# Handing out 32 DRAM-to-DRAM weight sums one at a time behind split weight operands

## The chip, the cores and the metric

The kernel runs on one core of one Trainium2 chip. The metric is the device time of one execution in microseconds (us); the figure quoted is the median of several executions.

## The reference, cut to what matters

The reference is one decoder layer with float32 weights: a normalised input projection (`w_in`), a causal 31-tap depthwise convolution with layer norm beside a multi-head latent attention of 8 heads, a gated merge and an output projection, a cross-attention on 256 memory tokens, and a squared-ReLU MLP, followed by a final RMS norm. The part that the change concerns is the second MLP product:

```python
u = rms_norm(h, norm_mlp_g[l])
h = h + jnp.square(jax.nn.relu(u @ w_mlp1[l])) @ w_mlp2[l]
```

`w_mlp2` has 4096 rows and 1024 columns. The kernel cuts it into four blocks B11, B12, B21, B22 (2048 rows by 512 columns each) and forms the product with seven block products instead of eight (a Strassen-Winograd scheme). For that it needs four sums of weight blocks, which it makes at run time.

## The kernel before, in words

**Matmuls.** Every float32 operand is split into a high and a low float32r part by `split` (lines 225 to 227): ScalarE (ACT) casts the high part, `wh`, and a second engine subtracts to get the low part, `wl`. `mm3` (lines 261 to 263) then issues three matmuls for each tile: high by high, high by low, low by high. A weight chunk is loaded by SP into one of two `raw` buffers (`raw`, line 362; usually 1 MB), and `prep` splits it piece by piece into one of three `wh`/`wl` pairs. The second engine of a weight split is `w_eng[0]`: VectorE (DVE) for chunk 1, GpSimd (POOL) from the second projection chunk to the cross-attention, and DVE again from the cross-attention's output projection on. `Pipe.unit` prepares the next unit's operand before it emits the matmuls of the unit before.

**Stages.** In the profiled execution TensorE (PE) works through: the start, in which `x` and the first weight chunk arrive (0 to 26 us); the projections `ag`, `cq`, `ckv` and 16 gate units, with the convolution's taps on DVE beside them (to 223); the attention (to 330); the merge's output projection, 8 units (to 375); the memory cross-attention (to 470); the first MLP product, 32 units (`m1`, to 650); and the seven block products (`m2`, to 825).

**The sums.** `b_sums_gen` (lines 322 to 342) makes the four sums X, V, Y, Z in DRAM, each in four pieces of 1 MB. For a piece c there are four copies from DRAM to DRAM and four DMAs with an accumulate: X = B12 + B11, V = B12 + B22, then Y = B11 + V and Z = B21 + Y. These are 32 DMAs of 1 MB on the queue of POOL, since POOL issues them. The `m2` stage reads X first, at 670.9 us.

**Order.** Only PE's order is that of the program text. The instructions of the other engines are ordered by a scheduler, which may take an instruction earlier than the text has it when nothing that it needs holds it back. The text asks for one sum DMA after each of the 8 units of the output projection and for two after each pass of the `m1` loop (`b_sums`, called at lines 1075 and 1266). The copies depend on no computed data and the accumulating DMAs only on earlier sum DMAs, and the scheduler has put all 32 among POOL's first instructions: the first two are issued at 1.4 and 2.1 us and the last at 172.5 us.

Of the kernel before, what the change touches and what calls it, by code (L numbers as in the profile page):

```python
# [14 lines left out]
F32 = mybir.dt.float32  # L15
# [4 lines left out]
ALU = mybir.AluOpType  # L20
# [3 lines left out]
P = 128  # L24
# [168 lines left out]
def _body(tc, a):  # L193
# [5 lines left out]
    gps = nc.gpsimd  # L199

    def pool(name, bufs=1, side=None, space=None):
        kw = dict(name=name, bufs=bufs, reuse_waits="tile")
        if side:
            kw["side"] = side
        if space:
            kw["space"] = space
        cm = tc.tile_pool(**kw)
        return cm, cm.__enter__()
# [5 lines left out]
    cst_cm, cst = pool("cst")  # L214
# [5 lines left out]
    def bank(tag="mm"):  # L220
        nonlocal ps
        return ps.tile([P, S], F32, tag=tag, name=tag, bufs=PB[tag])


    def split(hi, lo, src, eng=None):
        act.copy(hi, src)  # L226
        (eng or dve).tensor_tensor(lo, src, hi.bitcast(F32), op=ALU.subtract)  # L227
# [27 lines left out]
    def mm3(out, pairs, first=True, last=True, again=False):  # L255

        n = len(pairs)
        cols = out.shape[-1] / S
        for i, ((wh, wl), (ah, al)) in enumerate(pairs):
            kw = dict(skip_group_check=True) if again else {}  # L260
            pe.matmul(out, wh, ah, start=first and i == 0, stop=False, **kw)  # L261
            pe.matmul(out, wh, al, start=False, stop=False, **kw)  # L262
            pe.matmul(out, wl, ah, start=False, stop=last and i == n - 1, **kw)  # L263
            tick(cols)
# [48 lines left out]
    sums = {(n, c): spp.tile([P, 2048], F32, name="%s_%d" % (n, c)) for n in SUMS for c in range(4)}  # L313
# [4 lines left out]
    def chunk_hbm(i):  # L318
        n = stream[i][3] * len(stream[i][4])
        return a["weights"][offs[i]:offs[i] + P * n].rearrange("(p n) -> p n", p=P)  # L320

    def b_sums_gen():

        src = lambda *key: chunk_hbm(ch[key])
        b11, b22, b21 = ((lambda c, n=n: src("m2", n, c)) for n in (0, 3, 5))
        b12 = lambda c: src("b12", c)
        start = lambda c: [(("x", c), b12(c)), (("v", c), b12(c)), (("y", c), b11(c)), (("z", c), b21(c))]
        adds = lambda c: [(("x", c), b11(c)), (("v", c), b22(c)), (("y", c), sums["v", c]),
                          (("z", c), sums["y", c])]
        steps = [(start(c), False) for c in range(4)]  # L330
        for c in range(4):
            for d, s_ in start(c):
                gps.dma_start(out=sums[d], in_=s_)
                yield
            if c > 0:
                for d, s_ in adds(c - 1):
                    gps.dma_start(out=sums[d], in_=s_, accum_op=ALU.add, max_dma_last_dim=8192)
                    yield
        for d, s_ in adds(3):
            gps.dma_start(out=sums[d], in_=s_, accum_op=ALU.add, max_dma_last_dim=8192)  # L340
            yield

    b_gen = b_sums_gen()

    def b_sums(n):
        for _ in range(n):
            next(b_gen, None)

    def raw(*key):
        ci = ch[key]  # L350
        while issued[0] < len(stream) and issued[0] < ci + RAW_BUFS:
            i = issued[0]
            _, _, _, kt, cols = stream[i]
            n = kt * len(cols)
            t = wp.tile([P, 2048], F32, tag="raw", name="raw", bufs=RAW_BUFS)
            src = sums[stream[i][1], stream[i][2]] if stream[i][1] in SUMS else chunk_hbm(i)
            raws[i] = t[:, :n].rearrange("p (k m) -> p k m", k=kt)
            if i == 1:
                for sl in (slice(0, 128), slice(128, 256)):
                    dma(out=raws[i][:, :, sl], in_=src.rearrange("p (k m) -> p k m", k=kt)[:, :, sl])  # L360
            else:
                dma(out=t[:, :n], in_=src)
            issued[0] += 1
        return raws[ci]

    def whl(kt, cols):
        hi = wp.tile([P, 1024], F32R, tag="wh", name="wh", bufs=3)
        lo = wp.tile([P, 1024], F32R, tag="wl", name="wl", bufs=3)
        return tuple(t[:, :kt * cols].rearrange("p (k m) -> p k m", k=kt) for t in (hi, lo))

    def prep(key, k0=0, kt=None, c0=0, cols=128):

        r = raw(*key)
        kt = r.shape[1] if kt is None else kt
        hi, lo = whl(kt, cols)
        split(hi, lo, r[:, k0:k0 + kt, c0:c0 + cols], w_eng[0])
        return hi, lo

    w_eng = [dve]
# [100 lines left out]
    n = NT * 16  # L480
# [176 lines left out]
    for k in range(KD):  # L657
# [9 lines left out]
        for i, j in ((0, 0), (1, 0), (0, 1)):  # L667
            for b, c0 in ((fa, 0), (fg, 128)):
                pe.matmul(b, hl[i][:, k % 4, c0:c0 + 128], (uh, ul)[j][:, k, :],
                          start=k == 0 and i == j == 0, stop=k == KD - 1 and j == 1)  # L670
        tick(2.0)
    pipe.ahead(lambda: prep(("ag", 1), c0=0))
    x_stats()

# [121 lines left out]
    def qkt(tag):  # L796
        return at.tile([P, 2, S], F32R, tag=tag, name=tag, bufs=QB)
# [17 lines left out]
    def k_pair(p):  # L815
        b = bank()
        c = slice(128 * p, 128 * p + 128)
        mm3(b, [((wkk[:, 0, k, c], wkk[:, 1, k, c]), (ckh[:, k, :], ckl[:, k, :])) for k in range(2)])
        for e in range(2):
            n = slice(64 * e, 64 * e + 64)  # L820
            rr = slice(64 - 64 * e, 128 - 64 * e)
            kt_ = qkt("k")
            split(kt_[n, 0, :], kt_[n, 1, :], b[n, :])
            act.copy(kt_[rr, 0, :], krh[rr, :].bitcast(F32))
            act.copy(kt_[rr, 1, :], krl[rr, :].bitcast(F32))
            ks[2 * p + e] = kt_
# [51 lines left out]
        return prep(("co", p // 2), c0=256 * (p % 2), cols=256)  # L878

    hq = None  # L880
    k_pair(0)
    for t in range(NT):
        b = bank()
# [182 lines left out]
    def out_unit(m):  # L1066
        def main(hl):
            b = bank()
            mm3(b, [(lhs(hl, k), (mgh[:, k, :], mgl[:, k, :])) for k in range(KD)])
            n1.add(m, b)  # L1070
        pipe.unit(lambda: prep(("wo", m // 2), c0=128 * (m % 2)), main)

    for m in range(KD):
        out_unit(m)
        b_sums(1)
        if m == 2:
            mem_norm()
    for m in range(XH):
# [174 lines left out]
    def spill(m):  # L1253
        b = bank("at")
        for t in range(NT):
            pe.transpose(b[:, t * P:(t + 1) * P], ht[:, m, t * P:(t + 1) * P], ident)
        t_ = hop.tile([P, NT, P], F32, tag="spill", name="spill", bufs=2)
        act.copy(t_.rearrange("p t c -> p (t c)"), b)
        act.dma_start(out=hsp[:, m * P:(m + 1) * P].rearrange("(t p) c -> p t c", p=P), in_=t_)

    for p in range(16):
        for j in range(2):
            m1_unit(p, j)
        if 1 <= p <= KD:
            spill(p - 1)
        b_sums(2)


    m2w = {}
# [215 lines left out]
```

## Time and profile before

| | |
|---|---|
| Median of 3 executions | 829.14 us (828.45 to 829.21) |
| The profiled execution, its own time | 826.94 us |
| Its span (first to last instruction) | 825.0 us |
| PE busy | 769.2 us (93%) |
| DVE busy | 537.8 us (65%) |
| ACT busy | 400.4 us (49%) |
| POOL busy | 175.1 us (21%) |
| Moved by DMA | 129.58 MB, 33.56 MB of it on POOL's queue |

PE is busy for 93% of the span, so what can be won lies in the 56 us in which it is not, and in stretches in which it works at its lower clock. The page's second part shows the span in 40 equal slices of 20.6 us each: one line per engine, the clock granted to PE, the load of the 16 DMA engines and what they moved. A release (`<-`) behind an idle time names the work that ended it.

### The profile page before, as it was taken

The numbers are of one execution on the slowest core, as the hardware profiler recorded it, in microseconds if no ns is written. First come the engines' busy times: TensorE is split into PE (matmuls) and PEld (weight loads), VectorE is DVE, ScalarE is ACT, GpSimd is POOL, SyncE is SP. The second block draws the span as 40 slices with busy tenths as digits, with TensorE's granted clock in tenths as the row PEclk, the third lists the DMA queues.
The fourth block names the chain that finished last, engine by engine and source line by source line (L and its number), as shares of the span: only waits on it lengthen the run. The fifth ranks groups of instructions, "written<-read, shape, count | busy, mean of one in ns | idle before, by whom it ended". The sixth has DMA issues, their size and how long they took to land.

```text
span 825.0 us, 9536 instructions
## 1 busy us (share of the span) xinstructions
PE 769.2 (93%) x3594; PEld 632.5 (77%) x3594; DVE 537.8 (65%) x808; ACT 400.4 (49%) x681; POOL 175.1 (21%) x120
## 2 busy tenths in 40 slices
PE   5889974889999999899899999999999999999995
PEld 3679764777878888688887888888888878888884
DVE  3988977583378885976778663333333376677785
ACT  4432231236876653633446554444344455555563
POOL 3646271643322221434632000000000000000000
PEclk7999998899999999999999999999999999999999
DMA  8899999971220214421422123322322355555564
GB/s 296 334 257 325 307 294 220 253 210 52 90 89 1 103 52 147 160 91 66 150 103 102 51 103 128 122 87 110 115 103 102 121 186 203 177 210 200 187 220 154
DMA packets 27645, 129.58 MB, mean 157 GB/s; under 512 B 2640, under 2 KB 10192, under 8 KB 16208
## 3 DMA queue, kind: packets, MB, share of 16 engines
q1 hardware_dynamic: 16048, 85.37, 28.9%
q0 software_dynamic: 2816, 33.56, 15.3%
q10 hardware_dynamic: 8736, 10.06, 3.8%
q8 instruction: 28, 0.46, 0.2%
q14 instruction: 17, 0.14, 0.1%
HBM read 124.78 MB, written 37.75 MB: 197 GB/s over the span
## 4 chain that ended last, share of the span: by engine, by line
PE 66%; DVE 12%; issue 8%; DMA 7%; ACT 4%; POOL 3%; SPq 0%; POOLq 0%; DVEq 0%; ACTq 0%
PE mm L263 18%; PE mm L262 18%; PE mm L261 18%; DMA v<-weights 3%; PE at L262 2%; PE at L263 2%; PE at L261 2%; POOL wl L227 2%; DMA raw<-weights 2%; DMA xr<-xT 1%; DVE q L227 1%; DVE mt L964 1%; ACT wh L226 1%; PE at L857 1%; DVE wl L227 1%
## 5 line engine op out<-in xcount | busy, mean ns | idle before, releaser
L226 ACT CAST wh<-raw 128x1024 fp32r<-128x1024 f32 (+4 forms) x146 | 147.5, 1013 | 278.8 <-PE mm L262 148.8
L227 POOL TENSOR_TENSOR wl<-raw,wh 128x1024 fp32r<-128x1024 f32 (+4 forms) x65 | 148.5, 2300 | 211.6 <-ACT wh L226 208.4
L227 DVE TENSOR_TENSOR wl<-raw,wh 128x1024 fp32r<-128x1024 f32 x81 | 98.9, 1223 | 132.0 <-ACT wh L226 132.0
L261 PE MATMUL mm<-hgh,wh 128*128 128x512 f32 x288 | 113.2, 393 | 0.0
L262 PE MATMUL mm<-hgl,wh 128*128 128x512 f32 x288 | 112.2, 389 | 0.0
L263 PE MATMUL mm<-hgh,wl 128*128 128x512 f32 x288 | 112.2, 389 | 0.0
L263 PE MATMUL mm<-uh,wl 128*128 128x512 f32 x176 | 72.0, 409 | 12.6 <-POOL wl L227 9.8
L541 DVE SCALAR_TENSOR_TENSOR cv<-zpad,vec,cv 128x512 f32<-128x512 f32 x116 | 80.0, 746 | 0.1
L261 PE MATMUL mm<-uh,wh 128*128 128x512 f32 x176 | 72.4, 411 | 0.0
L262 PE MATMUL mm<-ul,wh 128*128 128x512 f32 x176 | 70.7, 402 | 0.0
L263 PEld LDWEIGHTS mm<-hgh,wl 128*128 128x128 f32 x288 | 54.1, 188 | 11.5
L262 PEld LDWEIGHTS mm<-hgl,wh 128*128 128x128 f32 x288 | 54.1, 188 | 10.9
L261 PEld LDWEIGHTS mm<-hgh,wh 128*128 128x128 f32 x288 | 54.1, 188 | 10.9
L263 PEld LDWEIGHTS mm<-uh,wl 128*128 128x128 f32 x176 | 34.5, 196 | 22.6 <-POOL wl L227 11.5
L1280 POOL MEMSET eps<- 128x1 f32 x1 | 0.1, 99 | 215.7 <-PE mm L263 215.7
L263 PE MATMUL mm<-wh,hB 128*128 128x512 f32 x100 | 39.6, 396 | 1.1 <-DVE hB L227 1.1
L261 PEld LDWEIGHTS mm<-uh,wh 128*128 128x128 f32 x176 | 34.6, 197 | 7.6 <-issue 1.0
L261 PE MATMUL mm<-wh,hA 128*128 128x512 f32 x100 | 39.6, 396 | 0.9 <-ACT hA L226 0.9
L262 PEld LDWEIGHTS mm<-ul,wh 128*128 128x128 f32 x176 | 34.7, 197 | 7.1
L262 PE MATMUL mm<-wl,hA 128*128 128x512 f32 x100 | 39.5, 395 | 0.0
L262 PE MATMUL at<-wl,hA 128*128 128x512 f32 x72 | 28.6, 397 | 0.3 <-DVE wl L227 0.3
L261 PE MATMUL mm<-mgh,wh 128*128 128x512 f32 x64 | 26.0, 406 | 3.1 <-ACT mgh L226 3.1
(384 smaller groups left out, 1696.1 us busy)
## 6 DMA issues: line engine op xcount, KB each, us to landing
raw<-weights SPq DMA_DIRECT2D x55, 1024.0 KB, 4.9
x<-weights POOLq DMA_DIRECT2D x4, 1024.0 KB, 18.7
v<-weights POOLq DMA_DIRECT2D x4, 1024.0 KB, 18.6
y<-v POOLq DMA_DIRECT2D x4, 1024.0 KB, 9.2
z<-y POOLq DMA_DIRECT2D x4, 1024.0 KB, 9.7
raw<-x SPq DMA_DIRECT2D x4, 1024.0 KB, 4.8
raw<-y SPq DMA_DIRECT2D x4, 1024.0 KB, 4.9
raw<-v SPq DMA_DIRECT2D x4, 1024.0 KB, 4.8
```

Source lines behind the costliest of these rows:

```text
L226: act.copy(hi, src)
L227: (eng or dve).tensor_tensor(lo, src, hi.bitcast(F32), op=ALU.subtract)
L261: pe.matmul(out, wh, ah, start=first and i == 0, stop=False, **kw)
L262: pe.matmul(out, wh, al, start=False, stop=False, **kw)
L263: pe.matmul(out, wl, ah, start=False, stop=last and i == n - 1, **kw)
L541: dve.scalar_tensor_tensor(run if w < CW - 1 else acc[:, c, :], zs, wcol, run, op0=ALU.mult, op1=ALU.add)
L857: pe.transpose(b[:, (t - k) * P:(t - k + 1) * P], ptok[h, t][:, k * P:(k + 1) * P], ident)
L964: dve.tensor_tensor(t, t, gates[:, m, :], op=ALU.add)
L1280: gps.memset(eps, EPS)
```

## The change

A one-element copy on POOL, `pace`, now stands ahead of every sum DMA. It reads an element of the `wl` that was just split, so it cannot run before that split, and `issue_after` puts the DMA behind the copy in POOL's order. `b_sums` is now called by `prep` after each split and counts up by `b_rate`: nothing before the attention, one DMA for every two splits from the attention on, and one for every split in `m1` but the first, whose operand is prepared ahead of the loop. Copies and accumulating DMAs are interleaved one by one, each accumulation a round later than the copy that it adds to, and V is added ahead of X.

```diff
-        adds = lambda c: [(("x", c), b11(c)), (("v", c), b22(c)), (("y", c), sums["v", c]),
+        adds = lambda c: [(("v", c), b22(c)), (("x", c), b11(c)), (("y", c), sums["v", c]),
                           (("z", c), sums["y", c])]
-        steps = [(start(c), False) for c in range(4)]
-        for c in range(4):
-            for d, s_ in start(c):
-                gps.dma_start(out=sums[d], in_=s_)
-                yield
-            if c > 0:
-                for d, s_ in adds(c - 1):
+        for c in range(5):
+            for n in range(4):
+                if c < 4:
+                    d, s_ = start(c)[n]
+                    gps.dma_start(out=sums[d], in_=s_)
+                    yield
+                if c > 0:
+                    d, s_ = adds(c - 1)[n]
                     gps.dma_start(out=sums[d], in_=s_, accum_op=ALU.add, max_dma_last_dim=8192)
                     yield
-        for d, s_ in adds(3):
-            gps.dma_start(out=sums[d], in_=s_, accum_op=ALU.add, max_dma_last_dim=8192)
-            yield
...
-    def b_sums(n):
-        for _ in range(n):
-            next(b_gen, None)
+    pace = cst.tile([P, 1], F32, name="pace")
+    b_rate, b_due = [0.0], [0.0]
+
+    def b_sums(lo):
+
+        b_due[0] += b_rate[0]
+        while b_due[0] >= 1.0:
+            b_due[0] -= 1.0
+            ins = gps.tensor_copy(pace, lo[:, 0, 0:1].bitcast(F32))
+            with tc.issue_after(ins.ins):
+                next(b_gen, None)
...
         split(hi, lo, r[:, k0:k0 + kt, c0:c0 + cols], w_eng[0])
+        b_sums(lo)
         return hi, lo
...
     hq = None
+    b_rate[0] = 0.5
     k_pair(0)
...
         out_unit(m)
-        b_sums(1)
...
+    b_rate[0] = 1.0
     for p in range(16):
...
-        b_sums(2)
```

Three places show what moves. The first is POOL's order in the projections, where `wl` of 128x768 belongs to `cq` and `wl` of 128x1024 to the gates. Before:

```order
L227 TENSOR_TENSOR wl<-raw,wh 128x1024 [waits PE_49,Activation_49]
L333 DMA x_82<-weights 16x16384 [waits DMASW2_49]
L227 TENSOR_TENSOR wl<-raw,wh 128x768 [waits DMAHW4_49,PE_49,Activation_49]
L337 DMA y_88<-v_84 128x2048 [waits DMASW3_49,DMASW1_49]
L333 DMA v_86<-weights 16x16384 [waits DMASW4_49]
L227 TENSOR_TENSOR wl<-raw,wh 128x768 [waits PE_49,Activation_49]
L337 DMA z_92<-y_88 128x2048 [waits DMASW5_49,DMASW3_49]
L227 TENSOR_TENSOR wl<-raw,wh 128x768 [waits DMAHW5_49,PE_49,Activation_49]
```

The same place after the change:

```order
L227 TENSOR_TENSOR wl<-raw,wh 128x1024 [waits PE_49,Activation_49]
L227 TENSOR_TENSOR wl<-raw,wh 128x768 [waits DMAHW4_49,PE_49,Activation_49]
L227 TENSOR_TENSOR wl<-raw,wh 128x768 [waits PE_49,Activation_49]
L227 TENSOR_TENSOR wl<-raw,wh 128x768 [waits DMAHW5_49,PE_49,Activation_49]
L227 TENSOR_TENSOR wl<-raw,wh 128x768 [waits Activation_49]
```

All sum DMAs are gone from here, and with them the waits on other sum DMAs (`DMASW`) that stood between two weight splits. The second place is POOL's order at the end of the output projection and in the memory keys (`xk`), after the change; before, only the `wl` rows stood there:

```order
L351 COPY pace<-wl 128x1 [waits Pool_49]
L338 DMA y_88<-v_84 128x2048 [waits DMASW5_49,DMASW2_49]
L227 TENSOR_TENSOR wl<-raw,wh 128x1024 [waits DMAHW7_49,PE_49,Activation_49]
L227 TENSOR_TENSOR wl<-raw,wh 128x1024 [waits PE_49,Activation_49]
L351 COPY pace<-wl 128x1 [waits Pool_49]
L334 DMA z_93<-weights 16x16384
L227 TENSOR_TENSOR wl<-raw,wh 128x1024 [waits DMAHW0_49,PE_49,Activation_49]
L227 TENSOR_TENSOR wl<-raw,wh 128x1024 [waits PE_49,Activation_49]
L351 COPY pace<-wl 128x1 [waits Pool_49]
L338 DMA z_92<-y_88 128x2048 [waits DMASW3_49,DMASW1_49]
L227 TENSOR_TENSOR wl<-raw,wh 128x1024 [waits DMAHW1_49,PE_49,Activation_49]
```

Between two sum DMAs there are two weight splits, and a sum that needs another one (`z_92` needs `y_88`) stands two DMAs behind it. In all, 16 sum DMAs now stand among POOL's weight splits and 16 behind splits that DVE makes. The third place is SP's order at the start. Before:

```order
L360 DMA raw<-weights 128x8x128 [waits DMAHW7_49]
L470 DMA kon<-konst 128x576 [waits DMAHW0_49]
L471 DMA posi<-positions 128x4 [waits DMAHW1_49]
L362 DMA raw<-weights 128x2048 [waits DMAHW2_49,DMAHW3_49,DVE_49,Pool_49]
L362 DMA raw<-weights 128x2048 [waits DMAHW7_49,DMAHW6_49,DVE_49]
```

After the change:

```order
L366 DMA raw<-weights 128x8x128 [waits DMAHW7_49]
L368 DMA raw<-weights 128x2048 [waits DMAHW0_49,DMAHW3_49,DVE_49,Pool_49]
L477 DMA kon<-konst 128x576 [waits DMAHW1_49]
L478 DMA posi<-positions 128x4 [waits DMAHW2_49]
L368 DMA raw<-weights 128x2048 [waits DMAHW7_49,DMAHW6_49,DVE_49]
```

The constants (`kon`) and the positions, from which DVE computes the rotary tables, now stand behind a weight load that waits until the first `raw` buffer is free.

## Rows read from the trace of the kernel before

**Rows 1.** The page's second part: tenths in 40 slices of 20.6 us
```profile
PE   5889974889999999899899999999999999999995
...
PEclk7999998899999999999999999999999999999999
DMA  8899999971220214421422123322322355555564
GB/s 296 334 257 325 307 294 220 253 210 52 90 89 1 103 52 147 160 91 66 150 103 102 51 103 128 122 87 110 115 103 102 121 186 203 177 210 200 187 220 154
```

**Rows 2.** The page's DMA queues (packets, MB, engine share) and issues (KB, median landing)
```profile
q1 hardware_dynamic: 16048, 85.37, 28.9%
q0 software_dynamic: 2816, 33.56, 15.3%
...
raw<-weights SPq DMA_DIRECT2D x55, 1024.0 KB, 4.9
x<-weights POOLq DMA_DIRECT2D x4, 1024.0 KB, 18.7
...
z<-y POOLq DMA_DIRECT2D x4, 1024.0 KB, 9.7
```

**Rows 3.** Timeline of POOL: start us, duration us, instruction, idle before it and releaser
```profile
1.44 0.67 POOL L333 DMA_DIRECT2D x<-weights  x1
...
22.99 0.52 POOL L333 DMA_DIRECT2D y<-weights  x1
...
81.20 1.34 POOL L337 DMA_DIRECT2D v<-weights  x1
...
141.76 0.81 POOL L337 DMA_DIRECT2D y<-v  x1 [19.00 <-DMA v<-weights]
```

**Rows 4.** Timeline of PE at the same place: start us, duration us, instruction
```profile
144.04 0.61 PE L262 MATMUL at<-wl,uh 128*128 128x288 f32 x1 [11.00 <-POOL wl L227]
```

**Rows 5.** The chain of waits, in order of time: start us, duration us, what
```profile
78.04 15.33 DMA raw<-weights
...
107.89 0.43 PE mm L261
...
111.46 0.23 PE mm L261
```

**Rows 6.** Three stretches of 10 us: stretch, length, busy us and instructions, PEclk, DMA, GB/s
```profile
100.00:110.00 10.00, 5.51 (x20) 3.99 (x19) 10.00 (x18) 5.03 (x8) 5.95 (x4) 0.88 0.92 233
140.00:150.00 10.00, 5.96 (x30) 5.96 (x30) 0.00 (x0) 0.54 (x1) 4.43 (x4) 0.57 1.02 213
180.00:190.00 10.00, 10.00 (x49) 8.25 (x48) 3.01 (x5) 3.66 (x5) 3.70 (x3) 1.00 0.47 182
```

**Rows 7.** Whole stages, same columns (PE, PEld, DVE, ACT, POOL busy)
```profile
44.00:223.00 179.00, 158.18 (x750) 133.50 (x749) 128.77 (x205) 68.70 (x117) 77.14 (x59) 0.94 0.81 226
330.00:375.00 45.00, 40.92 (x170) 32.32 (x169) 38.50 (x53) 22.91 (x36) 19.86 (x8) 0.96 0.33 120
375.00:440.00 65.00, 62.21 (x354) 53.88 (x353) 47.99 (x67) 30.31 (x58) 29.72 (x13) 1.00 0.28 98
470.00:650.00 180.00, 180.00 (x814) 149.02 (x813) 70.97 (x89) 81.30 (x143) 0.00 (x0) 1.00 0.30 106
```

**Rows 8.** Timelines of ACT, PE and DVE in the first 44 us
```profile
13.62 0.72 ACT L230 ACTIVATE uh<-xr,vec 128x512 fp32r<-128x512 f32 x1 [1.31 <-DMA xr<-xT]
14.39 1.22 PE L669 MATMUL mm<-uh,wh 128*128 128x512 f32 x2 [7.26 <-ACT uh L230]
...
39.07 3.11 DVE L273 TENSOR_TENSOR rs_t<-rs_t,rv 128x4 f32<-128x4 f32 x1
...
43.66 0.62 PE L295 MATMUL at<-kon,rx 128*128 128x128 f32 x4 [2.75 <-issue]
```

**Rows 9.** Timeline of DVE in the first MLP product: two weight splits in a row
```profile
502.84 1.22 DVE L227 TENSOR_TENSOR wl<-raw,wh 128x1024 fp32r<-128x1024 f32 x1 [4.72 <-ACT wh L226]
...
508.27 1.23 DVE L227 TENSOR_TENSOR wl<-raw,wh 128x1024 fp32r<-128x1024 f32 x1 [1.43 <-ACT wh L226]
```

## Prediction, made before the changed kernel ran

> **What bounds the kernel now.** I began with the page's slices. PE is the engine to watch, and it is full nearly everywhere except in the first nine slices, up to about 185 us [rows 1]. Exactly there the 16 DMA engines are full and move 210 to 334 GB/s; afterwards their load falls to a fifth or so. The queue table says what fills them: POOL's queue carries 33.56 MB, a quarter of all bytes, and all of it early [rows 2]. A 1 MB accumulation into X or V takes 18.7 us to land in this crowd, while the median weight load of 1 MB, taken over the whole kernel, needs 4.9 us.
>
> Next come the waits between engines, in two shapes. In the first, a weight load itself is late: one that the chain follows takes 15.33 us, from 78.04 on [rows 5]. In the second, POOL stands in its own queue: at 141.76 it issues Y = B11 + V after 19.00 us of waiting for V [rows 3], the split behind it in order is late, and PE resumes at 144.04 after 11.00 us without work [rows 4]. Whoever asks who is waiting for the sums themselves finds nobody: they are read only after 670 us.
>
> Last the price. From 44 to 223 us PE is busy for 158.18 of 179.00 us and its mean granted clock is 0.94 [rows 7]; from 180 to 190 us, with the sums over, it has no gap and runs at 1.00 [rows 6]. After a gap of some microseconds the granted clock is at the lower of its two levels, 1.2 instead of 2.4 GHz: from 107.89 matmuls of 512 columns step at 0.43 us, from 111.46 at 0.23 [rows 5].
>
> **The change, part by part.**
>
> *From 44 to 223 us.* All sum DMAs leave this stretch. The gaps are 179.00 - 158.18 = 20.8 us [rows 7]. To this come the recoveries at the lower clock: one lasts about 3.6 us (107.9 to 111.5), in which steps of 0.43 in place of 0.23 lose nearly half, 1.7 us [rows 5]. Between 90 and 180 us I count four such recoveries (two of them in the first two stretches of rows 6, with mean clocks of 0.88 and 0.57), so 4 x 1.7 = 6.8 us. The most that this stretch can give is 27.6 us. Is another engine next? DVE is busy for 128.8 us [rows 7], part of it held up by POOL, and PE would need 179.0 - 27.6 = 151 us, so DVE fits, if less loosely than it looks, as its work comes in bursts. POOL's 77.1 us shrink by some 28 DMA issues. I keep 3.6 us as left-over waits and take **24 us**. Ends: 14 (half stays, since DVE's bursts then end last) and 27.6.
>
> *The start.* Two sums are issued from 1.44 us on [rows 3], ahead of most of x. The second slice of x lets ACT start at 13.62 and PE at 14.39, after 7.26 us without work [rows 8]. Without those two megabytes x comes earlier. Against it stands SP's new order: the constants now wait behind a weight load that needs the first buffer free, and the rotary tables, the row statistics and the broadcast at 43.66 hang on them in DVE's order. That broadcast already cost PE 2.75 us, and one DVE step ahead of it took 3.11 us [rows 8] while POOL ran a split. The gain is between 0 (the constants take it all) and 7.26 + 2.75 = 10.0; I take the middle, **5 us**.
>
> *The 16 sums among POOL's weight splits (attention to cross-attention).* Each costs POOL an issue of 0.52 us for a copy or 0.81 us for an accumulation, plus the small `pace` copy, which no row shows; I put it at 0.15. That is 16 x (0.67 + 0.15) = 13 us of POOL time. POOL is busy for 19.9 of 45 us and 29.7 of 65 us in the two stages that hold most of them [rows 7], and the operand ring lets it work ahead, so most is hidden. If the cover were gone, all 13 would show. On the channel, a sum fills all 16 engines for 0.153 x 825 / 32 = 3.9 us and a weight load of 1 MB for 0.289 x 825 / 85.4 = 2.8 us [rows 2]. The output projection takes one of each for two units of 5.4 us, 6.7 of 10.8 us: loose. In the memory keys a unit has half the columns, so two loads and two sums, 13.4 us, meet some 11 us: loads can slip there by 2 to 3 us, in one or two places. What POOL waits for now is a sum two DMAs back, four splits earlier; behind it queue the splits of `xq`. I take 2 us for POOL and 2 us for the loads, **4 us lost**, between 0 and 21 (13 + 8).
>
> *The 16 sums behind DVE's splits (mostly `m1`).* Two splits there are 508.27 - 502.84 = 5.4 us apart [rows 9], and one sum follows each. In 10.9 us the channel gets one load and two sums, 2.8 + 7.8 = 10.6 us: as good as full, up from 0.30 [rows 7], for about 14 units. Then it empties again, near 550 us, and X is not read before 670. I cost this at nothing. The cover is that a weight load is asked for about two units before its split, against 4.9 us to landing [rows 2], and that PE has no gap there now [rows 7]. POOL does nothing else in this stage. If a `pace` copy is late, it holds one of the three `wl` buffers, and DVE's split three units on waits for it. The `pace` copies that run on after the last sum queue behind nothing.
>
> *The sum.* 24 + 5 - 4 = 25 us. The profiled execution took 826.94, so it would take 801.9; the median of the runs stands 2.2 us above it, which gives **804.1 us**.
>
> **The rivals.**
>
> 1. *The early waits go entirely and the new ones stay hidden.* For it: PE has no gap from 180 to 190 us although weights still stream. Against it: the broadcast's gap hangs on DVE, which the change relieves only in part. 27.6 + 7 - 1 = 33.6 us: about 796.
> 2. *Half of the early stage stays*, because DVE's bursts or a late constant take the place of the DMA. For it: DVE is at 10.00 of 10 us from 100 to 110 while PE stands [rows 6]. Against it: DVE has nothing to do in the largest gap (140 to 150). 14 + 5 - 4 = 15 us: 814.
> 3. *POOL's issues grow.* An issue took 0.52 us at 22.99 but 1.34 at 81.20 [rows 3], and a `pace` copy might have to sit out a DVE split of 1.23 us [rows 9]. Were all 16 so, POOL would lose 16 x (0.82 + 1.23) = 33 us more, among splits that PE waits for; with half of it on the path, 16 us go: 821. The Trainium skill speaks for this rival (SBUF — State Buffer, section "Who interferes with whom"): a DVE instruction with two SBUF inputs and a GpSimd instruction that reads SBUF exclude each other for a whole instruction. In its section "SBUF: two separate sides" it adds that a DMA issued by GpSimd can take about 3.1 us instead of 0.62 beside a DVE copy; 16 issues would then lose some 40 us by an estimate from that page. The trace does not bear out that size: none of the rows of POOL's issues is above 1.34 us. So I keep the rival small.
> 4. *Slower: the sums pace the first MLP product.* If a sum needs longer than a unit, POOL falls behind, the `pace` copies hold the `wl` buffers, and DVE and PE take the sums' pace. With 9.7 us for each, the landing time of Z += Y [rows 2], 14 units lose 14 x (9.7 - 5.4) = 60 us: 864. It turns slower than before from 5.4 + 25/14 = 7.2 us a sum. For it: the channel is as good as full there. Against it: a landing time is not a rate, as several sums are in flight at once, and the early stage passed 31 issues in 171 us (1.4 to 172.5), 5.5 us each, with the weights beside them.
> 5. *The sums do not move*, as the scheduler ignored the text before. Against it: POOL's order shows them moved, each behind a copy that needs the split's result. 829.
>
> **How the numbers follow.** The forecast of 804 gets 0.60, with a range of its own of 798 to 811; rivals 1 to 5 get 0.15, 0.14, 0.05, 0.04 and 0.02. The range of **793 to 816** takes in the forecast and rivals 1 and 2 with their unknowns. It leaves out rivals 3 to 5 and a little of the tails, 0.15 in all. A measurement of this kernel can tell about 0.2%, 1.7 us, from no change. Faster: the forecast and rivals 1 to 3 less a remnant, 0.93. Same: rival 5 and the remnant, 0.03. Slower: rival 4, 0.04.
>
> **What would show it.** Right: DMA load of 0.3 to 0.5 in the slices from 40 to 185 us; no wait of POOL on a sum between weight splits there; the attention's first matmuls near 194 instead of 223 us; the broadcast of `rx` at 36 to 41 us instead of 43.66; PE at clock 1.00 from 100 to 180; and in `m1` a DMA load near 0.9 until about 530 us with PE still at 10.0 of 10. Wrong: PE gaps behind POOL's `wl` between the attention and the cross-attention, issues on POOL of 2 us or more, `wl` splits of DVE in `m1` that wait for `pace`, or a stretch from 44 us to the attention that still needs 165 us or more.

## The result, and the profile after

The changed kernel takes **803.21 us** (median of 4 runs, 802.75 to 803.36); the kernel before took 829.17 on the same chip. The ratio is 0.968, with a 95% interval of 0.967 to 0.970. The forecast was 804.1. The profiled execution took 803.36 us, its span is 801.3.

First, where the time went. PE does the same matmuls in the same order in both kernels, so the first matmul of a stage is a mark that can be compared:

| Stretch on PE | before | after | difference |
|---|---|---|---|
| start to the broadcast of `rx` | 43.7 | 35.3 | -8.4 |
| broadcast to the first matmul of the attention | 179.0 | 157.3 | -21.7 |
| attention | 118.6 | 119.0 | +0.4 |
| output projection to the first block product | 316.3 | 321.2 | +4.9 |
| block products to the end | 167.4 | 168.5 | +1.1 |
| span | 825.0 | 801.3 | -23.7 |

The second slice of x and the first two marks in the timeline of PE, after (start us, duration us, instruction, idle before it); [rows 8] has the first two of before, and the attention there began at 222.65:

```profile
9.59 0.74 PE L676 MATMUL mm<-uh,wh 128*128 128x512 f32 x2 [0.74 <-ACT uh L230]
35.28 1.08 PE L295 MATMUL at<-kon,rx 128*128 128x128 f32 x4 [4.79 <-issue]
192.55 0.40 PE L261 MATMUL mm<-ckh,wkk 128*128 128x512 f32 x1
```

The page's slices, after, which answer to [rows 1]:

```profile
PE   8799999999999998998999999999999999999995
PEclk9899999999999999899899999999999999999998
DMA  8213223223314248467645699995322455564663
GB/s 281 93 40 110 77 83 133 78 90 124 129 52 158 106 154 261 116 206 212 196 148 180 211 292 285 276 243 164 106 102 65 149 209 195 176 234 171 219 213 132
```

The DMA engines were full or nearly so in the first nine slices before; now they are lightly loaded there from the second slice on, and full in four later slices, from about 460 us on. PE's row has no digit under 8 between the second slice and the last. The same in stretches, after, with the columns of [rows 6, 7]:

```profile
44.00:193.00 149.00, 147.19 (x721) 123.05 (x720) 122.63 (x198) 65.06 (x112) 60.15 (x37) 1.00 0.26 90
470.00:530.00 60.00, 60.00 (x278) 49.68 (x277) 22.30 (x24) 27.05 (x48) 9.46 (x19) 1.00 1.02 281
```

PE stands still for 1.8 of 149 us in the early stretch, where it stood for 20.8 of 179 [rows 7], and the mean clock is 1.00 where it was 0.94. In these 60 us of `m1` the channel is as good as full, at 281 GB/s, and PE has no gap, although a weight load lands in 11.0 us (median) there instead of 5.0.

PE's longest waits, after (in total, times, longest):

```profile
PE at L295 <- issue: 4.8, 1, 4.8
PE at L295 <- DVE rr L274: 4.0, 1, 4.0
PE mm L261 <- ACT mgh L226: 3.1, 1, 3.1
PE mm L261 <- DVE sg L775: 1.8, 2, 1.1
```

No wait on POOL's `wl` is left among them; before, two groups of such waits led the list, with the 11.00 us of [rows 4] on top. The two longest are both behind chains of small DVE instructions: the broadcasts of `rx` and of `rr`. (For the first the view names no releaser; in the timeline DVE writes `rx` at 35.22, and PE starts at 35.28.) The timelines of DVE, POOL and PE, after, show what is in those chains:

```profile
24.62 4.81 POOL L227 TENSOR_TENSOR wl<-raw,wh 128x1024 fp32r<-128x1024 f32 x2
24.72 4.88 DVE L498 TENSOR_SCALAR ang<-kon,posf 128x16 f32<-128x16 f32 x4
...
371.55 0.84 POOL L338 DMA_DIRECT2D z<-y  x1 [0.33 <-issue]
371.99 5.47 DVE L227 TENSOR_TENSOR xkl<-xkt,xkh 128x256 fp32r<-128x256 f32 x1 [0.47 <-ACT xkh L226]
372.17 5.00 POOL L227 TENSOR_TENSOR wl<-raw,wh 128x1024 fp32r<-128x1024 f32 x2
...
382.37 1.11 PE L295 MATMUL at<-kon,rr 128*128 128x128 f32 x4 [4.03 <-DVE rr L274]
...
383.71 0.63 PE L262 MATMUL mm<-hgl,wh 128*128 128x512 f32 x1
384.14 0.63 PE L263 MATMUL mm<-hgh,wl 128*128 128x512 f32 x1
...
388.06 0.39 PE L261 MATMUL mm<-hgh,wh 128*128 128x512 f32 x1
388.29 0.39 PE L262 MATMUL mm<-hgl,wh 128*128 128x512 f32 x1
```

The same places before:

```profile
396.56 5.37 POOL L227 TENSOR_TENSOR wl<-raw,wh 128x1024 fp32r<-128x1024 f32 x2 [0.56 <-ACT wh L226]
...
400.49 1.72 DVE L227 TENSOR_TENSOR xkl<-xkt,xkh 128x256 fp32r<-128x256 f32 x1 [0.47 <-ACT xkh L226]
...
409.21 0.65 PE L295 MATMUL at<-kon,rr 128*128 128x128 f32 x4 [2.28 <-DVE rr L274]
```

One DVE instruction, `xkl`, takes 5.47 us in place of 1.72. In both kernels it ends 0.3 us behind a pair of POOL splits (377.46 and 377.17; 402.21 and 401.93), but before it met the tail of the pair and now the whole. Behind it the gap before `rr` is 4.03 instead of 2.28 us. After the gap PE runs at the lower of its clock levels, with steps of 0.43 us (383.71 to 384.14) that become 0.23 (388.06 to 388.29). Some ten matmuls pass so, where before there was none; and behind the gap early in the output projection, 3.1 us in both kernels, some 13 matmuls are slow now and 6 were before. Counted up: 1.75 us of longer gap and (10 + 7) x 0.2 = 3.4 us of slow matmuls make 5.15, against the 4.9 of the table. Only the longer gap can be put down to the sums; `e4_order_only` shows below that the slow matmuls come without any sum in this stretch.

### The profile page after: what moved, and what is told of

The parts are those of the page before. It is cut to its first block, busy times and chain, and to the rows that moved or that the text cites. A ratio compares the mean times of both kernels' runs of the same rounds, so it can differ in the third digit from the quotient of the medians.

```text
span 801.3 us, 9637 instructions
## 1 busy us (share of the span) xinstructions
PE 768.8 (96%) x3594; PEld 628.5 (78%) x3594; DVE 535.9 (67%) x808; ACT 400.9 (50%) x681; POOL 193.3 (24%) x169
## 4 chain that ended last, share of the span: by engine, by line
PE 76%; DVE 16%; ACT 3%; issue 3%; DMA 1%; SPq 0%; DVEq 0%; ACTq 0%
PE mm L263 21%; PE mm L261 21%; PE mm L262 21%; DVE cv L548 3%; PE at L262 3%; PE at L263 3%; PE at L261 3%; DVE q L227 1%; DVE mt L972 1%; DVE xkl L227 1%; DVE rs_t L272 1%; DMA xr<-xT 1%; PE at L864 1%; ACT wh L226 1%; DVE wl L227 1%
## 5 line engine op out<-in xcount | busy, mean ns | idle before, releaser
L227 POOL TENSOR_TENSOR wl<-raw,wh 128x1024 fp32r<-128x1024 f32 (+4 forms) x65 | 144.8, 2233 | 242.0 <-ACT wh L226 235.0
L263 PE MATMUL mm<-uh,wl 128*128 128x512 f32 x176 | 70.2, 399 | 0.5 <-DVE wl L227 0.5
L351 POOL COPY pace<-wl 128x1 f32<-128x1 f32 x49 | 16.8, 343 | 164.3 <-DVE wl L227 163.4
```

The lines of the kernel that those rows point to most:

```text
L351: ins = gps.tensor_copy(pace, lo[:, 0, 0:1].bitcast(F32))
```

## The experiments

All were measured beside the kernel before, and those of one group on one chip: the first group is `e1` to `e3` (before: 828.22), the second `e0_after_again` and `e5` to `e7` (827.35), the third `e4`, `e8`, `e6_again` and `e9` (828.39). This table has the stretches of each, with the columns of the table above:

| | start | to attention | attention | to block products | to end | median, ratio with interval |
|---|---|---|---|---|---|---|
| `e1_nosums` | 35.4 | 156.9 | 119.0 | 318.7 | 167.4 | 800.08, 0.966 [0.963, 0.970] |
| `e1b_pace_only` | 35.6 | 158.1 | 119.0 | 316.0 | 168.4 | 801.57, 0.968 [0.964, 0.971] |
| `e2_all_m1` | 35.4 | 157.8 | 119.0 | 316.6 | 173.0 | 803.80, 0.969 [0.964, 0.975] |
| `e3_paced_early` | 36.3 | 167.7 | 119.0 | 316.4 | 167.7 | 806.32, 0.974 [0.970, 0.978] |
| `e0_after_again` | 35.5 | 157.7 | 119.0 | 321.8 | 168.5 | 803.85, 0.970 [0.967, 0.974] |
| `e5_skip_mem` | 35.7 | 156.8 | 119.0 | 321.2 | 167.9 | 802.35, 0.968 [0.965, 0.971] |
| `e6_dve_ag2` | 32.5 | 156.7 | 119.0 | 321.2 | 167.6 | 797.73, 0.963 [0.960, 0.966] |
| `e7_both` | 32.9 | 155.5 | 119.0 | 320.4 | 168.5 | 797.96, 0.962 [0.958, 0.966] |
| `e4_order_only` | 44.0 | 179.9 | 119.0 | 319.2 | 167.8 | 829.38, 1.001 [0.999, 1.003] |
| `e8_half_early` | 36.9 | 158.4 | 119.1 | 321.0 | 167.6 | 803.57, 0.969 [0.966, 0.973] |
| `e6_again` | 32.3 | 157.1 | 119.0 | 321.3 | 167.6 | 797.58, 0.963 [0.959, 0.966] |
| `e9_dve_xk` | 32.4 | 155.5 | 119.0 | 318.2 | 167.6 | 794.76, 0.959 [0.955, 0.962] |

`e0_after_again` is the changed kernel itself, as the yardstick of its group. It and the first profile agree within 0.6 us in every stretch, so differences of a microsecond in one stretch say little. The stretch before the block products scatters more: `e4_order_only` has no sum in it, as the kernel before, and still takes 319.2 us against 316.3.

### What made the early gain: bytes, order or pace

**The pace alone.** All 32 sums in the early stretch, as before, but one behind each split:

```diff
-    b_rate, b_due = [0.0], [0.0]
+    b_rate, b_due = [1.0], [0.0]
...
-    b_rate[0] = 0.5
...
-    b_rate[0] = 1.0
```

> The pace copies stay, but at one sum per split from the start on, so that the same 32 MB move in the same stretch as before the change, now each behind a split and interleaved. If the load of the channel was the cost (sums and weights together ask for 3.9 + 1.4 us per split, against 5.6 us per unit of the gates but 4.2 and 3.2 us in cq and ckv), most of the gain is lost: 818 to 830 us. If the cost was POOL waiting in its own queue on sums issued shortly before, the interleaving removes most of it: 803 to 810 us.

Measured: 806.32 us, the attention begins at 204.0. Of the 30.1 us that the changed kernel gains to this mark, 18.6 come although all sums but the last are still issued ahead of it (the last at 206.83): 7.4 at the start, where the first two sums no longer go ahead of x, and 11.2 between the broadcast and the attention. POOL's waits on sums, `e3_paced_early`, 40 to 192 us (in total, times, longest), and the stretch itself:

```profile
POOL z L338 <- DMA y<-v: 4.7, 2, 2.6
```

```profile
40.00:192.00 152.00, 144.81 (x679) 120.55 (x679) 126.55 (x198) 56.81 (x101) 81.86 (x87) 0.96 0.89 256
```

The longest wait of POOL on a sum falls from the 19.00 us of [rows 3] to 2.6; the channel is still 0.89 busy. The median weight load in this stretch lands in 7.3 us, where it took 12.1 before. No wait of PE on POOL's `wl` is left. PE's longest waits from 38 to 205 us, and one of ACT:

```profile
PE at L578 <- ACT csT L528: 3.2, 1, 3.2
PE mm L261 <- DVE rs_t L272: 2.9, 2, 2.2
...
ACT wkk L226 <- DMA raw<-weights: 6.3, 1, 6.3
```

The longest can be followed to a late weight load: `csT` stands behind `wkk` in ACT's order, and `wkk` behind its load. The next is one of DVE's chains, as in the later sections.

**The order alone.** The new order of the sums without the copies that pace them:

```diff
-            ins = gps.tensor_copy(pace, lo[:, 0, 0:1].bitcast(F32))
-            with tc.issue_after(ins.ins):
-                next(b_gen, None)
+            next(b_gen, None)
```

> The order and the calls of the changed kernel, but without the pace copies and without the tie that puts a sum behind one: the scheduler puts all 32 sums among POOL's first instructions again, in the new interleaved order. Theory (what counts is that POOL does not stand in its own queue on a sum between two splits): the sums are bunched as before, POOL waits 10 us or more on a sum somewhere before 185 us, PE's gaps behind POOL's weight splits come back, the attention begins at 213 to 225 us, and the time is 818 to 829. Rival A (the interleaved order alone is what paced the early experiment): the attention begins at 202 to 206 and the time is 804 to 809. Rival B (it is all in the load of the channel): as rival A's 18.6 us could not have come from order or pace, the attention begins at 222 and the time is 829, with weight loads of about 12 us and no long wait of POOL.

Measured: 829.38 us, no change from before, and the attention begins at 223.9. The scheduler has put all 32 among POOL's first instructions again, the last at 171.98 us. The stretch, and POOL's waits in it, `e4_order_only`:

```profile
40.00:192.00 152.00, 130.09 (x599) 109.70 (x598) 114.51 (x189) 44.02 (x74) 73.17 (x60) 0.92 0.91 261
```

```profile
POOL z L338 <- DMA y<-v: 30.0, 3, 15.6
...
POOL y L338 <- DMA v<-weights: 7.2, 2, 4.9
```

The rate and the channel's load are those of `e3_paced_early` within 2%, and PE works 14.7 us less. So the theory held and both rivals fell: neither the order nor the load alone makes the loss. Without the pace, the sums bunch; then POOL waits up to 15.6 us in its own queue, and a weight load lands in 12.6 us instead of 7.3. These two go together in every run of this stretch, and which of them costs how much stays open. (In `m1` of the changed kernel, loads of 11.0 us cost PE nothing; but there DVE makes the splits, and POOL holds nobody up.)

**Half the density.** One sum for every two splits, from the first split on:

```diff
-    b_rate, b_due = [0.0], [0.0]
+    b_rate, b_due = [0.5], [0.0]
...
-    b_rate[0] = 0.5
...
-    b_rate[0] = 1.0
```

> The changed kernel with one sum for every two splits from the very first split on, and nothing else of the pacing: about half of the early bytes of the experiment with one sum per split, in the same stretch, with POOL's waits on sums shorter still. Theory (the part that was left there, 11.5 us to the attention, is the load of the channel): it shrinks with the load, so the attention begins at 195 to 199 us, and with the late loss of the sums that now stand before 650 us about as in the changed kernel the time is 802 to 808. Rival (what was left there was a fixed cost, such as POOL's issues or one load at the start): the attention begins at 202 to 204 again and the time is 805 to 810. If the load costs nothing at half density, the attention begins at 192 to 194 and the time is 800 to 804.

Measured: 803.57 us, the attention begins at 195.35, at the lower end of what the theory allowed. The stretch, `e8_half_early`:

```profile
40.00:192.00 152.00, 149.87 (x727) 124.91 (x726) 125.56 (x201) 63.66 (x111) 72.20 (x62) 0.99 0.56 178
```

At 0.56 of the channel, this stretch takes 1.2 us more from the broadcast to the attention than in the changed kernel (158.43 and 157.27), at 0.89 it took 10.5 more (167.75): about half of the bytes cost a ninth. A cost that is fixed, or that grows evenly with the sums, does not fit. That it is the load of the channel is argued: POOL's issues among its splits are halved too, and of PE's gaps in `e3_paced_early` only the one of 3.2 us was followed to a weight load. The time is that of the changed kernel. It was the density of the sums that had to change, more than their place.

### What was lost later

**No sums at all**, and **the copies without the sums**; in both the block products read weight blocks in place of the four sums:

```diff
-            src = sums[stream[i][1], stream[i][2]] if stream[i][1] in SUMS else chunk_hbm(i)
+            src = chunk_hbm(ch["m2", 0, stream[i][2]] if stream[i][1] in SUMS else i)
...
-    b_rate[0] = 0.5
...
-    b_rate[0] = 1.0
```

> The 32 sum DMAs and the pace copies are left out and the m2 stage reads plain weight blocks in their place, so the output is not the layer's. My theory: the change took 30 us off the time up to the attention and gave back 6 us after it (between the attention and the end of m1), through the sums. Without any sum the early part stays at an attention start of 192 us and the 6 us come back: 796 to 798 us. Rival: the 6 us given back have nothing to do with the sums (the clock after two gaps of PE): 802 to 804 us.

```diff
-            with tc.issue_after(ins.ins):
-                next(b_gen, None)
...
-            src = sums[stream[i][1], stream[i][2]] if stream[i][1] in SUMS else chunk_hbm(i)
+            src = chunk_hbm(ch["m2", 0, stream[i][2]] if stream[i][1] in SUMS else i)
```

> As the kernel after, with its pace copies at their places, but without the 32 sum DMAs (m2 reads plain weight blocks, so the output is not the layer's). It tells what the late loss of about 6 us is made of. If the one-element copies on POOL do it, by shifting POOL's splits against DVE's steps: 801 to 803 us. If the DMAs do it, by POOL's issue time or by the load of the channel: 796 to 799 us.

Measured: 800.08 and 801.57 us. The intervals are some 6 us wide and overlap with each other and with the changed kernel's, so the times alone don't settle it: by the ratios (0.966 and 0.968 against 0.968) the sums cost 0 to 2 us where they now stand. The stretches tell more: the one before the block products takes 318.7 without the copies and 316.0 with them. So the copies are not what costs there, although 801.57 lies in the range that was expected if they were. Both kernels have the same two gaps in it, 3.1 us at its beginning and 2.5 before `rr`. Two windows of each, `e1_nosums` first:

```profile
305.00:350.00 45.00, 41.22 (x165) 32.12 (x164) 35.36 (x49) 21.45 (x36) 19.68 (x9) 0.92 0.27 94
350.00:400.00 50.00, 47.52 (x266) 41.34 (x265) 34.72 (x46) 19.86 (x33) 23.11 (x11) 0.97 0.30 106
```

And `e1b_pace_only`:

```profile
305.00:350.00 45.00, 41.02 (x170) 32.25 (x169) 36.51 (x50) 22.53 (x37) 23.00 (x13) 0.96 0.26 94
350.00:400.00 50.00, 47.50 (x272) 41.34 (x271) 36.28 (x46) 20.76 (x36) 26.52 (x16) 1.00 0.30 106
```

PE is busy equally long, with fewer matmuls in the first kernel, whose mean clock is lower in both windows by 0.03 to 0.04, which is 45 x 0.04 + 50 x 0.03 = 3.3 us, about the 2.8 between them. The clock after a gap of the same length can come out either way, and no sum is needed for that. The changed kernel has 0.92 and 0.93 there.

`e4_order_only` says the same from the other side. From the output projection on its POOL does what it did before, with gaps of 3.1 and 2.48 us where before had 3.1 and 2.28; but some 13 and 6 matmuls are slow behind them, where before had 6 and none, and the stretch takes 319.2 us instead of 316.3. That is 2.9 of the changed kernel's 4.9 us without a single sum. In the kept profiles the two places go together: 5 or 6 slow matmuls behind the first gap and none behind the second in `before`, `e1b_pace_only`, `e2_all_m1` and `e3_paced_early` (316.0 to 316.6 us), 8 or more and 4 or more in all others (318.2 to 321.8). What decides between the two is open. What the sums cost in this stretch is then nearer 2 us than 5.

**All sums in the first MLP product**, none before it:

```diff
-    b_rate[0] = 0.5
...
-    b_rate[0] = 1.0
+    b_rate[0] = 1.1
```

> No sum before m1, then 1.1 sums per split there. My theory (the late loss arises among POOL's splits in the output projection and the memory keys; m1 can take the sums behind its own work): 797 to 799 us, with 32 sums in some 30 units, which fills the channel (32 x 3.9 us of sums and 16 x 2.8 us of loads = 170 us in 175). Rival 4 of the prediction (sums pace the first MLP product): DVE's splits wait for pace copies, PE gets gaps in m1, 805 to 830 us.

Measured: 803.80 us, no gain. The stretch before the block products falls to 316.6; how much of that is the sums' and how much the clock's, this run can't tell. But the block products take 173.0 instead of 168.5. POOL issues the last sum at 631.34, and PE waits early in the block products. That last issue, the longest wait of DVE from 560 to 680 us, and PE's waits from 628 to 700 us, `e2_all_m1`:

```profile
631.34 0.81 POOL L338 DMA_DIRECT2D z<-y  x1 [10.99 <-issue]
...
DVE wl L227 <- POOL pace L351: 12.1, 1, 12.1
...
PE mm L263 <- DVE hB L227: 2.8, 1, 2.8
PE mm L262 <- DVE wl L227: 1.6, 1, 1.6
```

This is the mechanism of rival 4, on a small scale: POOL stands on a sum, the `pace` copies behind it are late, and a DVE split waits 12.1 us for one of them. The changed kernel has no such wait, and PE waits 1.0 us for `hB` there. 32 sums are too many for `m1`: what is won before it is paid behind it.

**No sums in the memory keys.** My theory at this point was that the sum issued at 371.55 between two splits pushes the splits against `xkl`:

```diff
+    b_rate[0] = 0.0
     for m in range(XH):
         xk_unit(m)
```

> As after, but no sum is handed out in the memory cross-attention; m1 then carries 22 sums and ends them near 565 us. My theory: the largest late loss of the kernel after arises there, where POOL's pace copies and an issue shift two weight splits onto a DVE step (5.5 us in place of 1.7) ahead of the broadcast that PE waits for, and PE's clock falls after the 4.0 us gap. Without sums there the gap is 2.3 to 2.5 us again: 798 to 800 us, 3 to 5 us under the kernel after. Rival (the 2.5 us gap that remains also makes the clock fall, and sums in m1 cost what they saved): within 1.5 us of the kernel after.

Measured: 802.35 us, 1.5 less than the changed kernel beside it, inside both intervals, and the stretch still takes 321.2. The theory in this form fell: the gap before `rr` is still there, and another DVE instruction is the held one. The time is that of the rival, but not for its reason, as the gap did not shrink to 2.5 us. DVE, POOL and PE, `e5_skip_mem`:

```profile
367.86 2.42 POOL L227 TENSOR_TENSOR wl<-raw,wh 128x1024 fp32r<-128x1024 f32 x1 [0.39 <-ACT wh L226]
367.94 2.89 DVE L1038 TENSOR_TENSOR nacc<-nacc,nsq 128x512 f32<-128x512 f32 x1
...
382.21 1.12 PE L295 MATMUL at<-kon,rr 128*128 128x128 f32 x4 [4.21 <-DVE rr L274]
```

After, the same `nacc` took 0.68 us. That suggests that what matters is on which DVE instruction a POOL split happens to fall, and that the sums only shift it.

### Taking POOL's splits away from DVE's chains

**At the rotary tables.** DVE splits the third chunk, beside which the tables are computed, instead of POOL:

```diff
-        w_eng[0] = dve if c == 1 else gps
+        w_eng[0] = dve if c <= 2 else gps
```

> As after, but DVE makes the low parts of the third projection chunk, which POOL made. In the kernel after, DVE's small steps of the rotary tables stand for 4.9 us while POOL runs these two splits, and PE waits 4.8 us for the broadcast behind them and then works at the lower clock. If the two engines exclude each other there, the broadcast comes 2 to 4 us earlier and the run ends 2 to 5 us earlier, 798 to 801 us. Rival: DVE's own two splits of 1.2 us come ahead of the tables and the constants are late in any case: the same within 1 us.

Measured: 797.73 us, 6.1 under the changed kernel in its group. `ang` and the broadcast in the timelines of DVE and PE, `e6_dve_ag2`:

```profile
25.95 0.65 DVE L498 TENSOR_SCALAR ang<-kon,posf 128x16 f32<-128x16 f32 x4
...
32.45 0.97 PE L295 MATMUL at<-kon,rx 128*128 128x128 f32 x4 [1.86 <-issue]
```

The four `ang` instructions take 0.65 us instead of 4.88, although DVE now does two splits more, and the broadcast comes 3.1 us earlier. From there to the attention another 1.0 us is saved; the remaining 1.5 of the span is spread over later stretches in pieces no larger than their scatter. `e6_again`, in the third group, repeats it at 797.58:

> The kernel in which DVE splits the chunk that stands beside the rotary tables, once more, as the yardstick of the next run on the same chip: 796 to 799 us, the broadcast of rx at 32 to 33 us, the gap before the broadcast of rr about 2 to 4 us.

**Both**, this and no sums in the memory keys:

> Both edits, of e5 and e6. If the two losses are independent, their gains add: 794 to 798 us. If a clock that falls after one gap or the other decides, the sum is smaller.

Measured: 797.96 us, not to be told from `e6_dve_ag2`: leaving the sums out of the memory keys adds nothing that can be measured.

**At the memory keys too.** On top of `e6`, DVE splits the memory-key units and the first piece of `xq`; the sums keep their order:

```diff
+    w_eng[0] = dve
     for m in range(XH):
         xk_unit(m)
     pipe.ahead(lambda: prep(("xq", 0)))
+    w_eng[0] = gps
```

> That kernel, and in addition DVE instead of POOL makes the low parts of the memory-key units and of the first xq piece. The sums are issued at the same places. Theory (the gap before the broadcast of rr comes from DVE instructions that are held for the length of a POOL split, wherever the sums shift them): with no POOL split beside the statistics no DVE instruction there takes over 1.5 us, the gap falls from 4 to under 1.5 us, the half-clock matmuls behind it go, and the stretch from the output projection to the block products falls from 321.2 to 317 to 318.5 us; the time is 793 to 795. Rival (the gap is DVE's own work, and more splits on DVE lengthen it): five splits of 1.23 us more, the gap is 4 to 8 us, the time 798 to 803. If the sums' place in POOL's order were the cause, the gap would stay at 4 and the time at 797.

Measured: 794.76 us, the best of all, and 2.8 under `e6_again` beside it. The two intervals overlap, but the slowest execution of the one (794.89) is faster than the fastest of the other (795.96). Of the span, 3.1 us go in the stretch before the block products, 321.3 to 318.2, which is about as much as this stretch scatters; the gap itself is the firmer sign. It falls from 4.0 to 2.3 us only, not under 1.5, and some six slow matmuls stay behind it: two instructions of the chain are still held, now by the splits of the next `xq` pieces. POOL, DVE and PE, `e9_dve_xk`:

```profile
369.52 2.39 POOL L227 TENSOR_TENSOR wl<-raw,wh 128x1024 fp32r<-128x1024 f32 x1 [3.66 <-ACT wh L226]
369.57 2.37 DVE L273 TENSOR_TENSOR rs_t<-rs_t,rv 128x4 f32<-128x4 f32 x1
...
372.21 0.54 POOL L334 DMA_DIRECT2D x<-weights  x1
372.38 2.77 DVE L272 SCALAR_TENSOR_TENSOR rs_t<-rr 128x4 f32<-128x4 f32 x1
372.76 2.37 POOL L227 TENSOR_TENSOR wl<-raw,wh 128x1024 fp32r<-128x1024 f32 x1
...
375.60 0.82 PE L295 MATMUL at<-kon,rr 128*128 128x128 f32 x4 [2.31 <-DVE rr L274]
```

Instructions on 128x4 elements, which take 0.16 us elsewhere in the chain, take 2.37 and 2.77 and end at 371.94 and 375.15; the splits end at 371.91 and 375.13. With the sums in the same order and the gap smaller, it was the splits and not the sums' place that held DVE there. A version with the other `xq` splits on DVE as well wasn't tried.

## Why the prediction was right, and where it was not

The time came out 0.9 us from the forecast. The terms did not come out so well: they missed by +3.4, -2.3 and -2.4 us, and the sum was good because these partly cancel, to -1.3. The rest of the closeness is luck too: the forecast set the median 2.2 us above the profiled execution, as before, but after the change it stands 0.15 below it. The profiled execution took 803.36 us where 801.9 had been worked out. Of the signs named, two lay just outside: the DMA load of the early stretch at 0.26 (0.3 to 0.5 expected) and the broadcast at 35.28 (36 to 41).

*From 44 us to the attention: 24 predicted, 21.7 measured.* Mechanism and size were right. The two shapes of waiting that the prediction named, late loads and POOL in its own queue, were not weighed against each other, and their common cause was not named: the bunching of the sums. `e4_order_only` and `e3_paced_early` show it, with the same bytes in the same stretch and 12.2 us between them from the broadcast on. The step "All sum DMAs leave this stretch." was credited with the whole gain; `e8_half_early` gets all but 1.2 us of it with half of the sums still there. One count was off, without effect on the sum: 23 sum DMAs were issued in this stretch before, not some 28.

*The start: 5 predicted, 8.4 measured.* This term was mis-sized, as a middle between ends. The second slice of x lets PE start at 9.59 us after 0.74 without work, instead of 14.39 after 7.26 [rows 8]. `e3_paced_early`, with its first sum at 22.56 us, keeps 7.4 of the 8.4, so this gain comes from the sums that were issued before x had arrived. Its first issue in the timeline of POOL, `e3_paced_early`:

```profile
22.56 0.67 POOL L334 DMA_DIRECT2D x<-weights  x1
```

The constants behind a weight load were not the price, since their load was issued at 15.40 us instead of 16.58: DVE's chain was late because `ang` was held for 4.88 us, as `e6_dve_ag2` shows. The row on which the prediction had seen this in the kernel before, a 3.11 us step beside a split, was the right one to look at [rows 8].

*The sums among POOL's splits: 4 predicted, 6.4 measured* (0.4 + 4.9 + 1.1). The size is near, the mechanism was wrong: "2 us for POOL and 2 us for the loads". No PE wait on a POOL split is left, and one load of 9.4 us in the memory keys held nobody up. What was lost is DVE held behind a POOL split, and the lower clock after two gaps. The held instruction shows as 1.75 us of longer gap. The clock's share, 2.9 us in `e4_order_only`, comes without any sum in the stretch, so it is not shown to be the sums' doing, and that the term came near is luck.

*The sums in `m1`: nothing predicted, nothing measured.* The channel is full for 60 us without a gap on PE. POOL waits for a sum only at the end; its last two issues and the group of the `pace` copies, after:

```profile
521.80 0.82 POOL L338 DMA_DIRECT2D y<-v  x1 [2.50 <-DMA v<-weights]
535.74 0.81 POOL L338 DMA_DIRECT2D z<-y  x1 [10.13 <-DMA y<-v]
```

```profile
L351 POOL COPY pace<-wl 128x1 f32<-128x1 f32 x49 | 16.8, 343 | 164.3 <-DVE wl L227 163.4
```

No DVE split waits for a `pace` copy there, so rival 4 fell, and the 535.7 of the last issue is near the 550 that was worked out. A `pace` copy takes 0.34 us and not 0.15, which is 3 us more for 16 of them; in `e1b_pace_only`, with the copies alone, the stretch before the block products takes 316.0 us, so they are hidden. With all 32 sums in `m1` the wait that rival 4 described did occur, as `e2_all_m1` shows.

*The other rivals.* Rival 1 (796) would need the early waits and the new ones gone; the early ones did nearly go, to 1.8 us of gaps, but the late loss of 6.4 took it back. Rival 2 fell with the same row: DVE's bursts don't end last once the bunching is over. Rival 3: the issues of the sums take 0.51 to 0.87 us, less than the 1.34 of before. The sentence of the Trainium skill on a GpSimd DMA that takes 3.1 us beside a DVE copy (SBUF — State Buffer, section "SBUF: two separate sides") is borne out by no issue in any run here; the longest took 1.88 us, in `e2_all_m1`. Rival 5 fell with the first profile; `e4_order_only` shows that the text alone would have moved nothing, and that the pace copies did it.

## What to carry to other kernels

When background transfers slow a kernel, look first at how densely they are issued and not only at where: a scheduler that may take an instruction early will bunch all those that depend on nothing, and a one-element copy that reads a value of the foreground work paces them. In the early stretch half of the channel's time cost next to nothing and nine tenths cost 10.5 us; in `m1` a full channel cost nothing, so a share alone does not say what it costs. And before giving elementwise work to POOL, look which chains of small DVE instructions run beside it: here two and then five splits of 1.23 us more on DVE cost less than the POOL splits of 2.4 us that held it (6.1 and 2.8 us gained, the second near the scatter).

## What the runs showed of the hardware that was not expected

- A DVE instruction that meets a POOL split can end with it, however small it is: 128x4 elements in 2.37 and 2.77 us instead of 0.16, `xkl` in 5.47 instead of 1.72 or 0.42. The Trainium skill has this as a rule for a DVE instruction with two SBUF inputs beside a GpSimd instruction that reads SBUF (SBUF — State Buffer, section "Who interferes with whom"): the engine that comes second waits for the whole instruction of the first. The trace agrees with it in size and end, to 0.03 us in `e9_dve_xk`. How `xkl` came to sit out two splits in a row, 5.47 us, no run here shows. The prediction had cited the rule for POOL's sake; it was DVE that paid, and PE behind it. Twice the DVE instruction began a little ahead of the split that it then sat out (371.99 and 372.17 after; 372.38 and 372.76 in `e9_dve_xk`); POOL was issuing a sum at both moments (371.55 for 0.84 us, 372.21 for 0.54). That an issue holds DVE too would fit, but was only seen twice and not tried.
- The 16 DMA engines were busy throughout for 60 us of `m1`, at 281 GB/s, with weight loads of 11.0 us, and PE lost nothing. In the early stretch before, a share of 0.81 with bunched sums and loads of 12.1 us went with 20.8 us of gaps.
- Gaps of 2.5 us in front of the same matmuls were followed by four matmuls at the lower clock in `e1_nosums`, by some six in `e4_order_only` and by none in `e1b_pace_only`. Between kernels that do the same there, this made a stretch of 316 us up to 2.9 us longer.
